# RMSNorm with swish on one core: load and store pieces regrouped at the start and the end

## Chip, cores and metric

One core of a Trainium2 chip. The metric is device microseconds of that core; most runs of a kernel lie within 0.3% of each other.

## The reference

```python
def reference(x, gamma, eps):            # x: [16, 1024, 512] float32, gamma: [512]
    rms = np.sqrt(np.mean(x ** 2, axis=-1, keepdims=True) + eps)
    x_norm = x / rms * gamma
    return (x_norm * (1.0 / (1.0 + np.exp(-x_norm)))).astype(np.float32)
```

16,384 rows of 512 floats (2 KB) go in and out: 33.55 MB each way. Spread over 128 partitions, that is 128 rows per partition; "a load of 16 rows" below means 16 rows in each partition, 4.19 MB in all.

## The kernel before

Data goes through a ring of 96 rows per partition. SyncE issues the loads, ScalarE the stores. Compute goes in chunks of 4 rows: ScalarE squares, VectorE (DVE) sums, GpSimd (POOL) makes the reciprocal root, VectorE normalises, ScalarE applies the swish in place, and the rows are stored from there. A load waits only for the stores of the rows whose place it takes.

```python
sizes = [4, 4, 8] + [16] * 6 + [8, 8]     # rows per partition of each tile: load = store
ring = 96
early = 2                                 # loads issued ahead of everything else
cn = 4                                    # rows per chunk
...
def dram(ap, t):                          # a tile is one contiguous block of HBM
    first, sz, _ = tiles[t]
    return ap[first : first + P * sz].rearrange("(p n) d -> p n d", n=sz)
...
def load(t):
    _, sz, at = tiles[t]
    ...                                   # waits: stores of tiles that held this place
    return nc.sync.dma_start(out=buf(t), in_=dram(xf, t)).then_inc(ld[t], 16)
...
def square(k):                            # ScalarE, chunk k
    t, at, first = chunks[k]
    if first:
        nc.scalar.wait_ge(ld[t], 16)      # the tile's load has landed
    ...
def store(t):
    need(
        nc.scalar.dma_start(out=dram(of, t), in_=buf(t)), s_swish, ends[t]
    ).then_inc(st[t], 16)
...
for k in range(K + 3):                    # ScalarE's program order
    if k < K:
        square(k)
    while stored < T and ends[stored] <= k - 2:
        store(stored)
        stored += 1
    if 2 <= k < K + 2:
        swish(k - 2)
```

Of the kernel before, what the change touches and what calls it, by code (L numbers as in the profile page):

```python
# [8 lines left out]
@with_exitstack  # L9
def kernel(  # L10
    ctx: ExitStack,
    tc: tile.TileContext,
    x: bass.AP,
    gamma: bass.AP,
    eps: bass.AP,
    out: bass.AP,
):
    nc = tc.nc
    P = nc.NUM_PARTITIONS
    AF = mybir.ActivationFunctionType  # L20
    ALU = mybir.AluOpType
    fp32 = mybir.dt.float32
    bf16 = mybir.dt.bfloat16

    xf = x.flatten_outer_dims()
    of = out.flatten_outer_dims()
    R, D = xf.shape


    sizes = [4, 4, 8] + [16] * 6 + [8, 8]  # L30
    ring = 96
    early = 2
    cn = 4
    n_sq = 3
    N = sum(sizes)
    assert N * P == R, (N, R)


    tiles = []
    done = 0  # L40
    for sz in sizes:
        assert done % ring + sz <= ring
        tiles.append((done * P, sz, done % ring))
        done += sz
    T = len(tiles)

    chunks = [
        (t, r, r == at)
        for t, (_, sz, at) in enumerate(tiles)
        for r in range(at, at + sz, cn)  # L50
    ]
    K = len(chunks)
    ends = []
    e = 0
    for sz in sizes:
        e += sz // cn
        ends.append(e)

    inv_d = 1.0 / float(D)
    eps_f = float(eps)  # L60



    tc.close()
    tc.compile()  # L65

    def sbuf(name, shape, dt=fp32):
        return nc.alloc_sbuf_tensor(name, shape, dt).ap()

    xb = sbuf("xb", [P, ring, D])  # L70
    gamma4 = sbuf("gamma4", [P, D])
    gamma_sb = sbuf("gamma_sb", [P, D])
    junk = [sbuf(f"junk{i}", [P, D], bf16) for i in range(2)]
    neg_half = sbuf("neg_half", [P, cn])
    ms = sbuf("ms", [P, K, cn])
    aeps = sbuf("aeps", [P, K, cn])
    rstd = sbuf("rstd", [P, K, cn])
    sq = [nc.alloc_psum_tensor(f"sq{i}", [P, 4, D], fp32).ap() for i in range(2)]

    ld = [nc.alloc_semaphore(f"ld{t}") for t in range(T)]  # L80
    st = [nc.alloc_semaphore(f"st{t}") for t in range(T)]
    scratch = nc.dram_tensor("scratch", [P, 16], fp32, kind="Internal").ap()
    blank = sbuf("blank", [P, 16])
    s_blank = nc.alloc_semaphore("s_blank")
    s_scratch = nc.alloc_semaphore("s_scratch")
    s_gld = nc.alloc_semaphore("s_gld")
    s_zero = nc.alloc_semaphore("s_zero")
    s_half = nc.alloc_semaphore("s_half")
    s_gamma = nc.alloc_semaphore("s_gamma")
    s_acc = nc.alloc_semaphore("s_acc")  # L90
    s_sq = nc.alloc_semaphore("s_sq")
    s_sum = nc.alloc_semaphore("s_sum")
    s_eps = nc.alloc_semaphore("s_eps")
    s_rstd = nc.alloc_semaphore("s_rstd")
    s_norm = nc.alloc_semaphore("s_norm")
    s_swish = nc.alloc_semaphore("s_swish")

    def need(ins, sem, value):
        return ins.wait_op(sem, value, "sem-ge")

    def dram(ap, t):
        first, sz, _ = tiles[t]
        return ap[first : first + P * sz].rearrange("(p n) d -> p n d", n=sz)

    def buf(t):
        _, sz, at = tiles[t]
        return xb[:, at : at + sz, :]


    stored_by_sync = set()  # L110

    def load(t):
        _, sz, at = tiles[t]
        waits = [
            u for u in range(t)
            if tiles[u][2] < at + sz and at < tiles[u][2] + tiles[u][1]
            and u not in stored_by_sync
        ]
        for u in waits:
            nc.sync.wait_ge(st[u], 16)  # L120
            stored_by_sync.add(u)
        return nc.sync.dma_start(out=buf(t), in_=dram(xf, t)).then_inc(ld[t], 16)

    entry = nc.main_func.blocks[0].instructions
    here = nc.cur_bb.bb.instructions
    for t in range(early):
        ins = load(t).ins
        assert here[-1] is ins or here[-1].name == ins.name
        here.pop()
        at = next(  # L130
            i for i, other in enumerate(entry)
            if other.engine == mybir.EngineType.SP
            and isinstance(other, mybir.InstDrain)
        )
        entry.insert(at, ins)
    for t in range(early, T):
        load(t)
    nc.sync.wait_ge(s_scratch, 16)


    nc.gpsimd.memset(blank, 0.0).then_inc(s_blank, 1)  # L141
    nc.gpsimd.memset(gamma4, 0.0).then_inc(s_zero, 1)  # L142
    nc.gpsimd.memset(neg_half, -0.5).then_inc(s_half, 1)  # L143
    nc.gpsimd.wait_ge(s_half, 1)
    for k in range(K):
        need(
            nc.gpsimd.tensor_scalar(  # L147
                out=aeps[:, k, :], in0=ms[:, k, :], scalar1=eps_f, scalar2=None,
                op0=ALU.add,
            ),  # L150
            s_sum, k + 1,
        ).then_inc(s_eps, 1)
        need(
            nc.gpsimd.tensor_tensor(  # L154
                out=rstd[:, k, :], in0=aeps[:, k, :], in1=neg_half, op=ALU.pow
            ),
            s_eps, k + 1,
        ).then_inc(s_rstd, 1)


    def square(k):
        t, at, first = chunks[k]
        if first:
            nc.scalar.wait_ge(ld[t], 16)
        acc = nc.scalar.activation(  # L165
            out=junk[k % 2], in_=xb[:, at + n_sq, :], func=AF.Square,
            scale=inv_d**0.5, accum_out=ms[:, k, n_sq : n_sq + 1],
        )
        if k >= 2:
            need(acc, s_acc, k - 1)  # L170
        acc.then_inc(s_acc, 1)
        square = nc.scalar.activation(  # L172
            out=sq[k % 2][:, 0:n_sq, :], in_=xb[:, at : at + n_sq, :],
            func=AF.Square, scale=inv_d**0.5,
        )
        if k >= 2:
            need(square, s_sum, k - 1)
        square.then_inc(s_sq, 1)

    def swish(k):  # L180
        _, at, _ = chunks[k]
        rows = xb[:, at : at + cn, :]
        need(
            nc.scalar.activation(out=rows, in_=rows, func=AF.Silu), s_norm, k + 1  # L184
        ).then_inc(s_swish, 1)

    def store(t):
        need(
            nc.scalar.dma_start(out=dram(of, t), in_=buf(t)), s_swish, ends[t]
        ).then_inc(st[t], 16)  # L190

    need(nc.scalar.dma_start(out=scratch, in_=blank), s_blank, 1).then_inc(
        s_scratch, 16
    )
    need(
        nc.scalar.dma_start(out=gamma4[0:P:32, :], in_=gamma.partition_broadcast(4)),
        s_zero, 1,
    ).then_inc(s_gld, 16)
    nc.scalar.preload_act_table_set("silu_and_others")  # L199
    stored = 0  # L200
    for k in range(K + 3):
        if k < K:
            square(k)
        while stored < T and ends[stored] <= k - 2:
            store(stored)
            stored += 1
        if 2 <= k < K + 2:
            swish(k - 2)


    def sums(k):
        need(
            nc.vector.tensor_reduce(  # L213
                out=ms[:, k, 0:n_sq], in_=sq[k % 2][:, 0:n_sq, :], op=ALU.add,
                axis=mybir.AxisListType.X,
            ),
            s_sq, k + 1,
        ).then_inc(s_sum, 1)

    def norm(k):  # L220
        _, at, _ = chunks[k]
        for j in range(cn):
            row = xb[:, at + j, :]
            ins = nc.vector.scalar_tensor_tensor(  # L224
                out=row, in0=row, scalar=rstd[:, k, j : j + 1], in1=gamma_sb,
                op0=ALU.mult, op1=ALU.mult,
            )
            if j == 0:
                need(ins, s_rstd, k + 1)
        ins.then_inc(s_norm, 1)  # L230

    for k in range(K + 1):
        if k < K:
            sums(k)
        if k == 0:
            need(
                nc.vector.stream_shuffle(gamma_sb, gamma4, [0] * 32), s_gld, 16  # L237
            ).then_inc(s_gamma, 1)
        if k == 1:
            nc.vector.wait_ge(s_gamma, 1)  # L240
        if k >= 1:
            norm(k - 1)


    for t in range(T):
        if t not in stored_by_sync:
            nc.sync.wait_ge(st[t], 16)

# [34 lines left out]
```

## Time and profile before

| | before |
|---|---|
| time | 160.27 us median of 3 (160.11 to 160.32) |
| span of the profiled run | 158.7 us |
| VectorE busy | 138.9 us, 87% |
| ScalarE busy | 125.3 us, 79% |
| moved | 67.15 MB, 423 GB/s over the span |
| loads / stores | 11 / 11 |
| last store | issued at 150.11, landed 8.6 us later |

Read the two limits together: VectorE runs without a gap from about 11 us on, but so do the DMA engines.

### The profile page before, as it was taken

The page shows a single profiled execution, that of the slowest core. Times are in us where ns is not written, and L with a number is a line of the kernel's source. Part 1 is how long each engine was busy: PE and PEld are TensorE (multiplying, and loading weights), DVE is VectorE, ACT ScalarE, POOL GpSimd, SP SyncE. Part 2 cuts the span into 40 slices and gives each one's busy share as a digit, 9 for nine tenths or more (in the row PEclk, how much of TensorE's full clock was granted, in tenths as well). Part 3 has the DMA queues.
Part 4 walks back from the last instruction along what each step waited for, and adds up shares of the span by engine and source line. Part 5 has one row for each costly group of instructions (what it writes and reads, how often), then busy time and mean ns, then how long its engine had stood idle before and what let it go on. Part 6 is the DMA issues. An engine that isn't in the chain of part 4 may idle for free.

```text
span 158.7 us, 439 instructions
## 1 busy us (share of the span) xinstructions
DVE 138.9 (87%) x162; ACT 125.3 (79%) x129; POOL 65.4 (41%) x71
## 2 busy tenths in 40 slices
DVE  0249999999999999999999999999999999999300
ACT  0935989888888889988888888888998888883600
POOL 2035444444455555544444445555544444445000
DMA  7999999999999999999999999999999999999997
GB/s 235 427 523 405 396 450 419 409 452 407 460 394 413 467 421 452 413 396 479 432 413 429 446 429 413 425 417 458 429 454 396 434 446 438 446 413 438 388 458 301
DMA packets 3324, 67.15 MB, mean 423 GB/s; under 512 B 501, under 2 KB 501, under 8 KB 505
## 3 DMA queue, kind: packets, MB, share of 16 engines
q1 hardware_dynamic: 1584, 33.56, 49.9%
q10 hardware_dynamic: 1736, 33.57, 49.3%
q14 instruction: 4, 0.02, 0.0%
HBM read 33.56 MB, written 33.56 MB: 423 GB/s over the span
## 4 chain that ended last, share of the span: by engine, by line
DVE 85%; DMA 5%; ACT 1%; issue 1%; POOL 0%; POOLq 0%
DVE xb L224 53%; DVE ms L213 32%; DMA gamma<-in_gamma_dram 5%; ACT xb L184 1%; DVE gamma_sb L237 0%; POOL gamma L142 0%; POOL blank L141 0%; POOLq L65 0%
## 5 line engine op out<-in xcount | busy, mean ns | idle before, releaser
L224 DVE SCALAR_TENSOR_TENSOR xb<-xb,rstd,gamma_sb 128x512 f32<-128x512 f32 x128 | 87.4, 748 | 0.0
L184 ACT ACTIVATE xb<-xb 128x2048 f32<-128x2048 f32 x32 | 61.1, 1909 | 17.8 <-DVE xb L224 17.8
L213 DVE TENSOR_REDUCE ms<-sq 128x3 f32<-128x1536 f32 x32 | 56.1, 1754 | 7.0 <-ACT sq L172 7.0
L147 POOL TENSOR_SCALAR aeps<-ms 128x4 f32<-128x4 f32 x32 | 20.6, 644 | 75.2 <-DVE ms L213 75.2
L172 ACT ACTIVATE sq<-xb 128x1536 f32<-128x1536 f32 x32 | 45.9, 1433 | 0.0
L154 POOL TENSOR_TENSOR rstd<-aeps,neg_half 128x4 f32<-128x4 f32 x32 | 44.0, 1376 | 2.7
L165 ACT ACTIVATE junk<-xb 128x512 bf16<-128x512 f32 x32 | 19.7, 615 | 3.4 <-DMA xb<-in_x_dram 3.3
L165 ACT ACTIVATION_READ_ACCUMULATOR junk<-xb 128x1 f32 x32 | 6.0, 186 | 0.0
L199 ACT ACT_TABLE_LOAD x1 | 1.3, 1283 | 3.6 <-issue 3.6
L237 DVE LOAD_MASK_SELECT gamma_sb<-gamma x1 | 0.0, 14 | 2.3 <-DMA gamma<-in_gamma_dram 2.3
L141 POOL MEMSET blank<- 128x16 f32 x1 | 0.1, 111 | 1.5 <-POOLq L65 1.5
L237 DVE STREAM_SHUFFLE gamma_sb<-gamma 128x512 f32<-128x512 f32 x1 | 0.7, 717 | 0.0
L142 POOL MEMSET gamma<- 128x512 f32 x1 | 0.5, 524 | 0.0
L264 POOL MEMSET const-float32-0.0<- 128x1 f32 x1 | 0.1, 98 | 0.2 <-issue 0.2
L264 POOL MEMSET const-bfloat16-1.0<- 128x1 bf16 x1 | 0.1, 102 | 0.0
L264 POOL MEMSET const-uint8-127<- 128x1 uint8 x1 | 0.1, 101 | 0.0
L143 POOL MEMSET neg_half<- 128x4 f32 x1 | 0.1, 101 | 0.0
L264 POOL MEMSET const-float32-1.0<- 128x1 f32 x1 | 0.1, 98 | 0.0
## 6 DMA issues: line engine op xcount, KB each, us to landing
xb<-in_x_dram SPq DMA_DIRECT2D x6, 4096.0 KB, 41.9
out_dram<-xb ACTq DMA_DIRECT2D x6, 4096.0 KB, 31.1
xb<-in_x_dram SPq DMA_DIRECT2D x3, 2048.0 KB, 35.0
out_dram<-xb ACTq DMA_DIRECT2D x3, 2048.0 KB, 10.7
xb<-in_x_dram SPq DMA_DIRECT2D x2, 1024.0 KB, 5.8
out_dram<-xb ACTq DMA_DIRECT2D x2, 1024.0 KB, 20.8
scratch<-blank ACTq DMA_DIRECT2D x1, 8.0 KB, 7.7
gamma<-in_gamma_dram ACTq DMA_DIRECT2D x1, 8.0 KB
```

What stands on the lines that cost most here:

```text
L141: nc.gpsimd.memset(blank, 0.0).then_inc(s_blank, 1)
L142: nc.gpsimd.memset(gamma4, 0.0).then_inc(s_zero, 1)
L147: nc.gpsimd.tensor_scalar(out=aeps[:, k, :], in0=ms[:, k, :], scalar1=eps_f, scalar2=None, op0=ALU.add,),
L154: nc.gpsimd.tensor_tensor(out=rstd[:, k, :], in0=aeps[:, k, :], in1=neg_half, op=ALU.pow),
L165: acc = nc.scalar.activation(out=junk[k % 2], in_=xb[:, at + n_sq, :], func=AF.Square, scale=inv_d**0.5, accum_out=ms[:, k, n_sq : n_sq + 1],)
L172: square = nc.scalar.activation(out=sq[k % 2][:, 0:n_sq, :], in_=xb[:, at : at + n_sq, :], func=AF.Square, scale=inv_d**0.5,)
L184: nc.scalar.activation(out=rows, in_=rows, func=AF.Silu), s_norm, k + 1
L199: nc.scalar.preload_act_table_set("silu_and_others")
L213: nc.vector.tensor_reduce(out=ms[:, k, 0:n_sq], in_=sq[k % 2][:, 0:n_sq, :], op=ALU.add, axis=mybir.AxisListType.X,),
L224: ins = nc.vector.scalar_tensor_tensor(out=row, in0=row, scalar=rstd[:, k, j : j + 1], in1=gamma_sb, op0=ALU.mult, op1=ALU.mult,)
L237: nc.vector.stream_shuffle(gamma_sb, gamma4, [0] * 32), s_gld, 16
L264: nc = _bacc.Bacc("TRN2", target_bir_lowering=False, num_devices=1)
```

## The change

The intent: fewer transfers. Rows are grouped as 8, 8 and seven times 16, and the pieces of loads and stores are listed apart from the groups. The first store moves 8 rows where it was two of 4; the last load moves 16 rows where it was two of 8. The first two loads (4 rows) and the last two stores (8 rows) keep their size, but are now pieces of a larger group, so in HBM each partition's piece lies at a pitch of 16 KB or 32 KB.

```diff
-    sizes = [4, 4, 8] + [16] * 6 + [8, 8]
+    groups = [8, 8] + [16] * 7
     ring = 96
+    loads = [(0, 0, 4), (0, 4, 4), (1, 0, 8)] + [(g, 0, 16) for g in range(2, G)]
+    stores = [(0, 0, 8), (1, 0, 8)] + [(g, 0, 16) for g in range(2, G - 1)]
+    stores += [(G - 1, 0, 8), (G - 1, 8, 8)]
     ...                                  # pieces are (group, first row, rows)
-    def dram(ap, t):
-        first, sz, _ = tiles[t]
-        return ap[first : first + P * sz].rearrange("(p n) d -> p n d", n=sz)
+    def dram(ap, piece):
+        g, r, n = piece
+        rows = ap[begin[g] * P : (begin[g] + groups[g]) * P]
+        return rows.rearrange("(p n) d -> p n d", n=groups[g])[:, r : r + n, :]
     ...
     def square(k):
-        t, at, first = chunks[k]
-        if first:
-            nc.scalar.wait_ge(ld[t], 16)
+        at, landing = chunks[k]          # the loads that this chunk is first to need
+        for i in landing:
+            nc.scalar.wait_ge(ld[i], 16)
```

The rest (cut) only carries the two lists through the ring waits, the semaphores and the final waits.

More of the change, by code (lines that the diff above doesn't have):

```diff
@@ L27 @@
     R, D = xf.shape
-    sizes = [4, 4, 8] + [16] * 6 + [8, 8]
+    groups = [8, 8] + [16] * 7
+    G = len(groups)
+    assert sum(groups) * P == R, R
+    begin = [sum(groups[:g]) for g in range(G)]
     ring = 96
+    loads = [(0, 0, 4), (0, 4, 4), (1, 0, 8)] + [(g, 0, 16) for g in range(2, G)]
+    stores = [(0, 0, 8), (1, 0, 8)] + [(g, 0, 16) for g in range(2, G - 1)]
+    stores += [(G - 1, 0, 8), (G - 1, 8, 8)]
     early = 2
@@ L34 @@
     n_sq = 3
-    N = sum(sizes)
-    assert N * P == R, (N, R)
-    tiles = []
-    done = 0
-    for sz in sizes:
-        assert done % ring + sz <= ring
-        tiles.append((done * P, sz, done % ring))
-        done += sz
-    T = len(tiles)
-    chunks = [
-        (t, r, r == at)
-        for t, (_, sz, at) in enumerate(tiles)
-        for r in range(at, at + sz, cn)
-    ]
-    K = len(chunks)
-    ends = []
-    e = 0
-    for sz in sizes:
-        e += sz // cn
-        ends.append(e)
+    chunks = []
+    new = list(range(len(loads)))
+    for g in range(G):
+        for c in range(0, groups[g], cn):
+            need_now = [
+                i for i in new if loads[i][0] == g and loads[i][1] < c + cn
+            ]
+            new = [i for i in new if i not in need_now]
+            chunks.append(((begin[g] + c) % ring, need_now))
+    assert not new
+    K = len(chunks)
+    ends = [-(-(begin[g] + r + n) // cn) for g, r, n in stores]
     inv_d = 1.0 / float(D)
@@ L78 @@
     sq = [nc.alloc_psum_tensor(f"sq{i}", [P, 4, D], fp32).ap() for i in range(2)]
-    ld = [nc.alloc_semaphore(f"ld{t}") for t in range(T)]
-    st = [nc.alloc_semaphore(f"st{t}") for t in range(T)]
+    ld = [nc.alloc_semaphore(f"ld{t}") for t in range(len(loads))]
+    st = [nc.alloc_semaphore(f"st{t}") for t in range(len(stores))]
     scratch = nc.dram_tensor("scratch", [P, 16], fp32, kind="Internal").ap()
@@ L99, in need, with buf, load @@
         return ins.wait_op(sem, value, "sem-ge")
-    def dram(ap, t):
-        first, sz, _ = tiles[t]
-        return ap[first : first + P * sz].rearrange("(p n) d -> p n d", n=sz)
-    def buf(t):
-        _, sz, at = tiles[t]
-        return xb[:, at : at + sz, :]
-    stored_by_sync = set()
-    def load(t):
-        _, sz, at = tiles[t]
-        waits = [
-            u for u in range(t)
-            if tiles[u][2] < at + sz and at < tiles[u][2] + tiles[u][1]
-            and u not in stored_by_sync
-        ]
-        for u in waits:
-            nc.sync.wait_ge(st[u], 16)
-            stored_by_sync.add(u)
-        return nc.sync.dma_start(out=buf(t), in_=dram(xf, t)).then_inc(ld[t], 16)
+    def dram(ap, piece):
+        g, r, n = piece
+        rows = ap[begin[g] * P : (begin[g] + groups[g]) * P]
+        return rows.rearrange("(p n) d -> p n d", n=groups[g])[:, r : r + n, :]
+    def buf(piece):
+        g, r, n = piece
+        at = (begin[g] + r) % ring
+        assert at + n <= ring
+        return xb[:, at : at + n, :]
+    stored_by_sync = set()
+    def load(i):
+        g, r, n = loads[i]
+        old = begin[g] + r - ring
+        for u, (h, q, m) in enumerate(stores):
+            if (
+                begin[h] + q < old + n and old < begin[h] + q + m
+                and u not in stored_by_sync
+            ):
+                nc.sync.wait_ge(st[u], 16)
+                stored_by_sync.add(u)
+        return nc.sync.dma_start(
+            out=buf(loads[i]), in_=dram(xf, loads[i])
+        ).then_inc(ld[i], 16)
     entry = nc.main_func.blocks[0].instructions
@@ L135 @@
         entry.insert(at, ins)
-    for t in range(early, T):
+    for t in range(early, len(loads)):
         load(t)
@@ L180, in swish @@
     def swish(k):
-        _, at, _ = chunks[k]
+        at, _ = chunks[k]
         rows = xb[:, at : at + cn, :]
@@ L188, in store @@
         need(
-            nc.scalar.dma_start(out=dram(of, t), in_=buf(t)), s_swish, ends[t]
+            nc.scalar.dma_start(out=dram(of, stores[t]), in_=buf(stores[t])),
+            s_swish, ends[t],
         ).then_inc(st[t], 16)
@@ L203 @@
             square(k)
-        while stored < T and ends[stored] <= k - 2:
+        while stored < len(stores) and ends[stored] <= k - 2:
             store(stored)
@@ L220, in norm @@
     def norm(k):
-        _, at, _ = chunks[k]
+        at, _ = chunks[k]
         for j in range(cn):
@@ L242 @@
             norm(k - 1)
-    for t in range(T):
+    for t in range(len(stores)):
         if t not in stored_by_sync:
```

## The prediction

> **What bounds the kernel now.** I read the page first for the busy shares, the memory rows and the chain that ended last. Then I asked for the landing of each transfer, and for the end of the timeline.
>
> The page of the kernel before:
>
> ```profile
> DVE  0249999999999999999999999999999999999300
> DMA  7999999999999999999999999999999999999997
> ...
> q1 hardware_dynamic: 1584, 33.56, 49.9%
> q10 hardware_dynamic: 1736, 33.57, 49.3%
> ...
> DVE 85%; DMA 5%; ACT 1%; issue 1%; POOL 0%; POOLq 0%
> ```
>
> The chain names VectorE (DVE, 85%), which runs without a gap from about 11 us to 148 us. But the DMA row is full in every slice, to the end. The two queues (q1 loads, q10 stores) fill 49.9 + 49.3 = 99.2% of 16 engines' 158.7 us. So two limits lie almost on one another, and the chain can name only one. Which one sets the end shows in the tail:
>
> ```profile
> 142.75 5.38 DVE L224 SCALAR_TENSOR_TENSOR xb<-xb,rstd,gamma_sb 128x512 f32<-128x512 f32 x8
> ...
> 148.17 1.91 ACT L184 ACTIVATE xb<-xb 128x2048 f32<-128x2048 f32 x1 [0.74 <-DVE xb L224]
> 150.11 0.34 ACTq L189 DMA_DIRECT2D out_dram<-xb  x1
> ```
> ```profile
> 144.00:148.00 4.00, 4.00 (x7) 1.91 (x1) 1.06 (x1) 1.00 0.96 414
> 148.00:152.00 4.00, 0.14 (x1) 1.91 (x1) 0.00 (x0) 1.00 0.95 406
> 152.00:156.00 4.00, 0.00 (x0) 0.00 (x0) 0.00 (x0) 1.00 1.06 455
> ```
>
> (The last columns of the second fence are the DMA share and GB/s.) The last store is issued at 150.11 and lands 8.6 us later, at 158.7. It carries 2.10 MB, which at 430 GB/s are 4.9 us. In the trace's packet records the store ahead of it is still moving until 153.4; only then does the last store get the engines, and its last packet ends at 158.3. A store into an empty queue would need some 1.5 to 2 us from issue to its first packet (the first load of all needs 1 us). So VectorE has a slack of about 3.3 - 1.8 = 1.5 us: **DMA throughput sets the end, VectorE is a close second.** 67.15 MB at the 430 GB/s of the middle of the run are 156 us, and the rest is start and receipt.
>
> **What the Trainium skill says.**
> - "DMA: Bandwidth & Descriptors", section "Where 436 GB/s comes from": the 16 ports together give 435 GB/s. The trace agrees: 421 to 441 GB/s in every stretch of 10 or 20 us between 30 and 140 us. So no cleverer order of transfers gains throughput.
> - Same page, "Queues, rings and completion order": each DMA engine goes round its queues packet by packet. Here a packet is one partition's row block: 1584 packets on q1 are 11 loads x (128 + 16 semaphore writes). So a queue with smaller packets gets a smaller share. Checked below against the landings, it agrees.
> - Same page, "Latency and other measured facts", HBM row pitch: pitches of 512 KiB and more, in powers of two, slow copies. The change makes the first two loads and the last two stores strided, with pitches of 16 and 32 KiB, far below that range; no run here shows yet what these cost.
>
> **The packet times, checked.** From the page, q10 moves 33.57 MB in 49.3% of 16 x 158.7 us, or 26.8 KB per us and engine: 0.31, 0.61 and 1.22 us for packets of 8, 16 and 32 KB (rows are 2 KB; 4, 8, 16 rows). An engine has 8 packets of each transfer. Alternating with 32 KB load packets a store of 4 rows takes 8 x (0.31 + 1.22) = 12.2 us, one of 8 rows 14.6, one of 16 rows 19.5. The first four stores, issued at 18.0, 22.5, 31.0 and 48.2:
>
> ```profile
> out_dram<-xb ACTq DMA_DIRECT2D x1, 1024.0 KB, 16.5
> out_dram<-xb ACTq DMA_DIRECT2D x1, 1024.0 KB, 25.0
> out_dram<-xb ACTq DMA_DIRECT2D x1, 2048.0 KB, 31.0
> out_dram<-xb ACTq DMA_DIRECT2D x1, 4096.0 KB, 33.1
> ```
>
> They land (last column, us after issue) at 34.5, 47.5, 62.0 and 81.3: spaced 13.0, 14.5, 19.3. The packet rule holds.
>
> **The change, part by part.**
>
> *Compute.* Nothing: 32 chunks of four rows, 128 normalising instructions of 748 ns, 32 sums of 1754 ns, the same waits between engines. No gain, no loss.
>
> *Start.* The same three first loads (4, 4, 8 rows), issued alike. Only the addresses of the first two are interleaved. VectorE's start hangs on gamma (landed at 11.0), which this does not touch. 0 us.
>
> *First store.* Two stores of 4 rows become one of 8, issued with the old second one at 22.5 instead of 18.0. Nothing idles meanwhile: the loads of the whole 96-row ring are queued by 4.9 us and the DMA row is full. But an 8-row packet gets a third of an engine where a 4-row one got a fifth. With the 4.3 us from issue to start that the first store showed, 22.5 + 4.3 + 14.6 = 41.4 us for the first landing, 56.0 for the second, against 62.0 for the same 16 rows before. The total rate is fixed, so the loads fall behind by what the stores gain: about 5.4 to 6 us of alternating.
>
> *Ring wait.* The load of rows 96 to 111 is issued when those stores land, so at 56 instead of 62. The load before it lands at about 82, so that wait was hidden, and stays hidden. 0 us.
>
> *Last load.* This is the part that could hurt. Before, the last three loads were
>
> ```profile
> xb<-in_x_dram SPq DMA_DIRECT2D x1, 4096.0 KB, 39.7
> ...
> xb<-in_x_dram SPq DMA_DIRECT2D x2, 2048.0 KB, 42.1
> ...
> xb<-in_x_dram SPq DMA_DIRECT2D x1, 2048.0 KB, 49.1
> ```
>
> (the middle line is the mean of the two small ones, 35.0 and 49.1). Issued at 62.1, 81.7 and 82.4, they land at 101.8, 116.7 and 131.5. The first 8 rows are wanted by ScalarE at 125.77 (its square of the 29th chunk), the other 8 at 134.4: slacks of 9 and 3 us. Now the 29th chunk waits for all 16 rows. The two small loads took 29.7 us, as 16 KB packets against 32 KB ones; one transfer of 32 KB packets takes 19.5, so it ends 10 us sooner, but the loads are 5.4 to 6 us late: 131.5 - 10.2 + 5.4 to 6 = **126.7 to 127.3**. My packet records give the same sum about 0.7 lower. ScalarE wants it at 125.77, and the VectorE sum behind it has another 0.33 us to spare (square ends 127.81, sum starts 128.14). So a stall of 0 to 1.2 us, most likely some 0.7 us.
>
> *End.* The last stores are of 16, 8 and 8 rows as before. A stall of 0.7 us moves the last issue from 150.1 to 150.8, inside the 1.5 us of slack. On the path: 0 us; if the load lands at 128.5 instead, some 2.4 - 1.5 = 0.9 us.
>
> *Packets.* One load and one store fewer: 2 x 144 = 288 packets of 3324, 18 per engine. In the packet records two 8 KB packets take 618 ns where one of 16 KB takes 611, two of 16 KB 1222 where one of 32 KB takes 1213, and a semaphore write 9. Saved per engine: 8 x 7 + 8 x 9 + 2 x 9 = 146 ns, on the path, as DMA sets the end: -0.15 us.
>
> Sum: 160.27 - 0.15 + a little for the chance of an unhidden stall (estimate 0.2) = 160.3 us.
>
> **The rivals.**
> 1. *The late last load becomes the bound.* For: the slack at its chunk falls from 9 us to about nothing. Against: the end has 1.5 us of slack, and its packets now take half of the engines, not a third. To cost 2% (3.2 us) it would have to land near 126.1 + 1.5 + 3.2 = 130.8, as late as all loads end now. Time then 161 to 163.
> 2. *Fewer, larger transfers gain.* For: DMA is the bound. Against: packets of 8 KB are already at full rate (0.309 us, 26.5 KB per us), and queues hide the fixed costs. At most 0.15 to 0.5 us: 159.8 to 160.1.
> 3. *The strided pieces or the later first store lose DMA time.* For: the first two loads meet an empty machine, and the last two stores are on the path. Against: packet lengths are unchanged, and the loads fill the gap. Ten per cent on the two last stores would be 1 us: 161.3.
>
> **Range and chances.** All that I can size lies between -0.5 and +1.2 us, and the three runs before lie within 0.2 us of each other. I take 159.7 to 161.4 as the range. Faster by 2% (157.1 us) would need over 435 GB/s on average: 1%. Slower by 2% (163.5) needs the worst case of rival 1 or something unseen: 2%. Within 2%: 97%.
>
> **What would show it.** DMA full in all slices again and about 430 GB/s in the middle; q1 with 1440 packets and q10 with 1592; first stores landing near 41 and 56; the last load landing near 127; a wait of ScalarE or VectorE of about a microsecond there, and VectorE ending near 149; the last store shorter from issue to landing by what VectorE lost (8.6 towards 7.9). It is wrong if the last load lands after 128.5, if the DMA row shows a hole near the end, or if the first or last slices move fewer GB/s than 235 and 301.

## The result

| | before | after |
|---|---|---|
| time, median | 160.27 us (160.11 to 160.32, 4 runs) | 160.34 us (160.24 to 160.80, 4 runs) |
| ratio | | 1.0011 (95%: 0.9991 to 1.0032) |
| span of the profiled run | 158.7 us | 158.9 us |

(Before has one more run here than in the table above.) A ratio is the mean time of one kernel's runs over that of the other's of the same rounds, so it isn't quite the ratio of the medians. The two kernels take the same time.

The page of the changed kernel: DMA busy tenths in 40 slices, the two queues (packets, MB, share of 16 engines), and the chain that ended last by engine.

```profile
DMA  7999999999999999999999999999999999999896
...
q1 hardware_dynamic: 1440, 33.56, 49.9%
q10 hardware_dynamic: 1592, 33.57, 49.1%
...
DMA 54%; DVE 34%; ACT 4%; issue 1%; POOL 0%; ACTq 0%; POOLq 0%
```

The DMA row is about as full as before, with the 288 packets fewer that were foretold. The chain now names DMA first, where it named VectorE with 85%. That looks like a new bottleneck and isn't: VectorE's busy time is 138.9 us in both. Near the end of the chain one chunk now waits for its load, so the walk back from the last instruction leaves VectorE there and follows the load and the stores behind it. A second trace of the same kernel (e11), with the same wait at the same chunk, names VectorE again:

```profile
DVE 83%; DMA 5%; ACT 4%; issue 1%; POOL 0%; another core or an unknown queue 0%; ACTq 0%; POOLq 0%
```

With two limits this close, the chain's shares tell which thread the walk picked up, not which limit holds.

That chunk in the timeline of the changed kernel (start, duration, engine, line, and in brackets the idle time before and what ended it), with the last store's issue:

```profile
126.33 0.63 ACT L169 ACTIVATE junk<-xb 128x512 bf16<-128x512 f32 x1 [0.33 <-DMA xb<-in_x_dram]
...
128.42 1.76 DVE L218 TENSOR_REDUCE ms<-sq 128x3 f32<-128x1536 f32 x1
...
150.40 0.34 ACTq L193 DMA_DIRECT2D out_dram<-xb  x1
```

ScalarE waits 0.33 us for the last load at the 29th chunk. VectorE's sum of that chunk starts at 128.42, where it was 128.14 before. But VectorE ran late before that: by 0.14 us at its first normalising (13.45, before 13.31) and by 0.08 us at the sum of the chunk ahead (123.91, before 123.83). So the late load costs it 0.2 us (0.21 in e11). The last store is issued 0.29 us later than before.

The first two stores and the last load of the changed kernel (KB, us from issue to landing):

```profile
out_dram<-xb ACTq DMA_DIRECT2D x1, 2048.0 KB, 19.4
...
out_dram<-xb ACTq DMA_DIRECT2D x1, 2048.0 KB, 26.2
...
xb<-in_x_dram SPq DMA_DIRECT2D x1, 4096.0 KB, 49.6
...
out_dram<-xb ACTq DMA_DIRECT2D x1, 2048.0 KB, 8.5
```

Issued at 22.47, 31.10 and 76.65, the first three land at 41.9, 57.3 and 126.2; foretold were 41.4, 56.0 and 126.7 to 127.3. The fourth line is the last store: 8.5 us, as against 8.6.

### The profile page after: what moved, and what is told of

It reads as the page before. It is cut to its first block, busy times and chain, and to the rows that moved or that the text cites. A ratio compares the mean times of both kernels' runs of the same rounds, so it can differ in the third digit from the quotient of the medians.

```text
span 158.9 us, 436 instructions
## 1 busy us (share of the span) xinstructions
DVE 138.9 (87%) x162; ACT 125.4 (79%) x129; POOL 90.1 (57%) x71
## 4 chain that ended last, share of the span: by engine, by line
DMA 54%; DVE 34%; ACT 4%; issue 1%; POOL 0%; ACTq 0%; POOLq 0%
DMA xb<-in_x_dram 31%; DVE xb L229 22%; DMA out_dram<-xb 18%; DVE ms L218 12%; DMA gamma<-in_gamma_dram 5%; ACT xb L188 2%; ACT sq L176 1%; ACT junk L169 0%; DVE gamma_sb L242 0%; POOL gamma L146 0%; POOL blank L145 0%; ACTq L168 0%; POOLq L64 0%
## 5 line engine op out<-in xcount | busy, mean ns | idle before, releaser
L151 POOL TENSOR_SCALAR aeps<-ms 128x4 f32<-128x4 f32 x32 | 50.5, 1577 | 50.9 <-DVE ms L218 50.9
L218 DVE TENSOR_REDUCE ms<-sq 128x3 f32<-128x1536 f32 x32 | 56.8, 1774 | 7.3 <-ACT sq L176 7.2
L158 POOL TENSOR_TENSOR rstd<-aeps,neg_half 128x4 f32<-128x4 f32 x32 | 38.8, 1212 | 2.7
```

The lines of the kernel that those rows point to most:

```text
L151: nc.gpsimd.tensor_scalar(out=aeps[:, k, :], in0=ms[:, k, :], scalar1=eps_f, scalar2=None, op0=ALU.add,),
L158: nc.gpsimd.tensor_tensor(out=rstd[:, k, :], in0=aeps[:, k, :], in1=neg_half, op=ALU.pow),
L218: nc.vector.tensor_reduce(out=ms[:, k, 0:n_sq], in_=sq[k % 2][:, 0:n_sq, :], op=ALU.add, axis=mybir.AxisListType.X,),
```

## The experiments

My theory: DMA throughput sets the end; the two queues share each DMA engine packet by packet, so packet sizes decide which queue runs ahead; and VectorE has a small slack at the end (time by which it may be late at no cost). Its rival: VectorE's chain sets the end, and a stall of it is paid in full. Landing times without a profile line below are those of the last semaphore write of a transfer in the trace's packet records, which are 0.4 to 1.1 us ahead of the landing in the profile.

### e1 to e4: the two parts apart, and the first store taken apart

e1 does the first part alone, e2 the second alone, e3 the second in the changed layout, e4 is e3 with both small stores held back:

```diff
 e1  groups = [8, 8] + [16] * 6 + [8, 8];  loads: (0,0,4), (0,4,4), then one per group;  stores: one per group
 e2  groups = [4, 4, 8] + [16] * 7;        loads: one per group;  stores: one per group, the last in two of 8
 e3  the changed kernel, with
-    stores = [(0, 0, 8), (1, 0, 8)] + ...
+    stores = [(0, 0, 4), (0, 4, 4), (1, 0, 8)] + ...
 e4  e3, and
+    ends[0] = ends[1]          # the first 4 rows wait for 8
```

> Only the first store is merged (8 rows at about 22.5 us); the last 16 rows are loaded as 8 and 8 again. My theory (queues share an engine packet by packet, DMA sets the end): the loads fall 5.1 us behind, as in the changed kernel (its last load ended at 125.8 in the packet records where 130.4 - 9.7 = 120.7 would be without it), so the very last load ends near 135.5 us instead of 130.4, ScalarE wants it at 134.4 and VectorE stalls about 1.3 us; the last store is issued near 151.4 instead of 150.1, which the drain of the store queue (it gets to the last store at 153.4) mostly hides: +0 to +0.3 us against before. Rival (VectorE's chain sets the end): the stall is on the path, +1.3 us or 0.8%.

> Only the last load is merged; stores of 4, 4, 8 rows at the start as before. My theory: the last load ends near 120.7 us in the packet records (130.4 - 9.7), some 5 us before ScalarE wants it, so no stall; VectorE ends at 148.2 as before; time within 0.2 us of before, about 0.1 us less for the fewer packets. Rival (a 16-row load in one transfer arrives later than two halves): a stall at the 29th chunk and a last issue after 150.1.

> The changed kernel with its first store split again into two of 4 rows (issued at 18.0 and 22.5), but with the changed layout: the first two loads and stores have 8 KB pieces at a pitch of 16 KB in HBM. Theory: a pitch costs nothing, so times and landings are those of e2 within 0.3 us (last load near 120.7). Rival (strided pieces cost DMA time): the first two loads land later than 4.5 and 6.9 us, or the whole is over 0.5 us slower than e2.

> As e3, but the first store of 4 rows waits for 8 rows, so both are issued at about 22.5. This parts the two halves of the first-store change: later, and in packets of 16 KB. Packet theory: the later start alone makes the stores 4 to 4.6 us later and the loads as much EARLIER, so the last load ends near 116.3 us, against 120.7 in e3 and 125.8 in the changed kernel. Rival (the later first store itself is what held the loads back): last load near or after 125.8. Time in both: within 0.3 us of before.

Measured, with 6 runs each and 11 of before on the same chip (median 160.36 us):

| | last load ends, expected | measured | time, median | ratio to before (95%) |
|---|---|---|---|---|
| e1 first store only | 135.5 | 135.9 | 160.86 | 1.0030 (0.9997 to 1.0062) |
| e2 last load only | 120.7 | 119.6 | 160.11 | 0.9982 (0.9954 to 1.0011) |
| e3 e2 in the changed layout | 120.7 | 121.1 | 160.44 | 1.0011 (0.9977 to 1.0046) |
| e4 e3, both stores late | 116.3 | 115.8 | 160.42 | 1.0003 (0.9970 to 1.0035) |
| before / changed kernel | | 130.4 / 125.8 | | |

Four landings, over a range of 20 us, come out within 1.1 us of what packet times, together with the landings of the two kernels, gave beforehand. e4 parts the first-store change in two: waiting longer brings the loads *forward* by 5.3 us (121.1 to 115.8); it's the 16 KB packets that push them back, by 10 us (115.8 to 125.8). The net of 4.7 us against e3 is what the prediction had as 5.4 to 6; e1 against before gives 5.5 for the same change.

Two expectations were missed in part. e3 was to match e2 within 0.3 us: its last load came 1.5 us later and its median is 0.33 us higher, and its first two loads ended at 4.80 and 7.31, past the 4.5 and 6.9 named for the rival (a cost of the pitch). The repeat of e2 (e12) ends its last load at 120.7, so a good part of the 1.5 us is scatter, and the intervals of e2 and e3 overlap: no cost of the pitch in time is shown, and one of a few tenths isn't excluded. In e2 VectorE ended at 148.91 and not at 148.2, because gamma landed late; its last store was issued at 150.88, 0.77 us later than before, and the span is still 158.8 us.

e1 is the stall test: the timeline of e1 at its 31st chunk, and its last issue.

```profile
136.30 0.63 ACT L168 ACTIVATE junk<-xb 128x512 bf16<-128x512 f32 x1 [1.54 <-DMA xb<-in_x_dram]
...
138.40 1.76 DVE L217 TENSOR_REDUCE ms<-sq 128x3 f32<-128x1536 f32 x1 [1.26 <-ACT sq L175]
...
151.74 0.34 ACTq L192 DMA_DIRECT2D out_dram<-xb  x1
```

VectorE stands still for 1.26 us (1.3 expected). The last store is issued at 151.74, yet lands 7.5 us after its issue instead of 8.6. In the packet records it follows the store ahead of it with no gap. The interval excludes the 0.8% of the rival, but e1's 0.3% can't be told from zero, nor from the 0.3 us that were allowed.

### e5: less VectorE work

```diff
-            row = xb[:, at + j, :]
+            row = xb[:, at + j, 0:384]
...
-                out=row, in0=row, scalar=rstd[:, k, j : j + 1], in1=gamma_sb,
+                out=row, in0=row, scalar=rstd[:, k, j : j + 1], in1=gamma_sb[:, 0:384],
```

> Wrong result on purpose: the changed kernel, but the normalising instructions work on 384 of 512 columns. VectorE loses some 0.17 us of each of 128 instructions, 20 us or more in all; ScalarE's work of about 3.9 us a chunk then paces the chunks at best. Theory (DMA throughput sets the end): same bytes, so the same time, between -0.7 and +1 us; the chunks now catch up with the loads and wait for them. Rival (VectorE's chain sets the end): 32 x 0.4 = 12 us or more faster.

Measured: 160.22 us against 160.13 of before, ratio 0.9986 (0.9935 to 1.0037). (The comparison with the reference let it pass: with this input gamma is 1 and the row factor near 1. It's still not the function wanted.) The page of e5, busy time and the rows of VectorE and DMA, then its 29th chunk from the timeline:

```profile
DVE 123.2 (78%) x162; ACT 124.5 (78%) x129; POOL 57.2 (36%) x71
...
DVE  0159978999999999999998499945999369997000
...
DMA  7999999999999999999999999999999999999896
```
```profile
126.25 0.63 ACT L169 ACTIVATE junk<-xb 128x512 bf16<-128x512 f32 x1 [3.64 <-DMA xb<-in_x_dram]
```

VectorE lost 15.7 us of work (138.9 to 123.2; I had expected 20 or more), and no gain in time shows (the interval reaches down to 1.0 us less). The work saved became holes in its row: ScalarE's squares waited 15.0 us for loads, in 7 places, against 3.9 us in the changed kernel. This is the clearest result: VectorE does not set the end. The rival wanted 12 us or more.

### e6: more bytes on the store queue

```diff
             store(stored)
+            if stored == 4:
+                nc.scalar.dma_start(out=extra,          # 1.05 MB, DRAM to DRAM
+                    in_=xf[0 : 4 * P].rearrange("(p n) d -> p (n d)", n=4),
+                ).then_inc(s_extra, 16)
```

> The changed kernel with 1.05 MB more on the store queue (a DRAM to DRAM copy of 8 KB per partition, issued behind the fourth store), on which nothing waits but the end. Theory (DMA has no idle time at all): 8 x 0.309 = +2.5 us. Rival (VectorE sets the end and DMA has room): below +1 us.

(In the kernel the copy stands behind the fifth store, not the fourth.) Measured: 163.10 us, ratio 1.0164 (1.0112 to 1.0216), that is +2.6 us (1.8 to 3.5), where 2.5 were expected. The first DMA engine to finish does so at 160.20 in the packet records, 157.63 in the changed kernel: +2.57. Within that interval, DMA time is paid one for one.

### e7 and e8: how much slack VectorE has

```diff
+        if k == K - 1:
+            for i in range(2):            # e8: range(6)
+                nc.vector.scalar_tensor_tensor(
+                    out=pad[:, i, :], in0=gamma_sb, scalar=rstd[:, 0, 0:1], in1=gamma_sb,
+                    op0=ALU.mult, op1=ALU.mult,
+                )
         for j in range(cn):
```

> The changed kernel with two more VectorE instructions of about 0.72 us ahead of the last four rows' normalising, which delays the last store's issue by 1.4 to 1.5 us, from 150.4 to 151.9. Theory: the store queue comes to the last store at 152.8 to 153.7 and a store needs 1.5 to 2 us from issue to first packet, so most of it is hidden: 0 to +0.6 us. Rival (the chain): +1.45 us, 0.9%.

> The same with six such instructions, 4.3 to 4.5 us: the last issue at about 154.8, well past the slack. Theory: +2.6 to +3.4 us, that is the delay less a slack of 1 to 1.8 us. Rival (the chain, no slack): +4.4 us.

Measured: e7 160.55 us, ratio 1.0013 (0.9965 to 1.0061); e8 162.15 us, ratio 1.0105 (1.0062 to 1.0147). e7 is hidden, as expected (the interval excludes the rival's 0.9%). e8 loses less than I expected: its span is 160.7 us, +1.8 on the changed kernel, not +2.6 to +3.4. The last store of e7, issued at 151.70, and that of e8, issued at 154.42:

```profile
out_dram<-xb ACTq DMA_DIRECT2D x1, 2048.0 KB, 7.3
```
```profile
out_dram<-xb ACTq DMA_DIRECT2D x1, 2048.0 KB, 6.3
```

Stretches of e8's tail (us, busy time of VectorE, ScalarE and GpSimd, then clock, DMA share and GB/s):

```profile
148.00:152.00 4.00, 4.00 (x7) 0.00 (x0) 0.00 (x0) 1.00 0.98 418
152.00:156.00 4.00, 0.45 (x1) 1.91 (x1) 0.00 (x0) 1.00 0.48 205
```

In e8 the queue has run empty (share 0.48), so 6.3 us is what this store takes when nothing stands before it. All above it is time spent in the queue, and so slack: 8.6 - 6.3 = 2.3 us before, 8.5 - 6.3 = 2.2 in the changed kernel, 1.2 left in e1, 1.0 in e7. e8's last issue is 4.02 us later than the changed kernel's, and 4.02 - 2.2 = 1.8 us is what it lost; that is the same two landings told once more, not a further check. A second way is: the store ahead ends at 153.43 (before) and 153.68 (changed kernel) in the packet records, and e8's last store needs 0.85 us from issue to first packet, so an issue up to 152.6 or 152.8 would have been in time. That is a slack of 2.4 to 2.5 us on the slowest engine.

### e9: the last load in four pieces, a miss

```diff
-    ... + [(g, 0, 16) for g in range(2, G)]
+    ... + [(g, 0, 16) for g in range(2, G - 1)]
+    loads += [(G - 1, r, 4) for r in (0, 4, 8, 12)]
```

> The opposite of the change's last load: the last 16 rows come in four loads of 4 rows (8 KB packets) in place of one of 16. Same bytes. Packet theory: against 32 KB store packets each of the four takes 8 x (0.31 + 1.22) = 12.2 us, so from 106.5 us they end near 118.7, 130.9, 143 and 151 (the last one sooner, as the stores run out of data), where ScalarE wants them at 126, 130.3, 134.7 and 139: VectorE stalls by some 12 us in all, the DMA row shows a hole near the end, and the time is 8 to 11 us longer. Rival (smaller pieces can be used sooner, the order of bytes is what counts): no stall, time within 0.5 us.

Measured: 161.08 us against 160.44 of before, ratio 1.0005 (0.995 to 1.0061); not 8 to 11 us longer. The pieces end at 119.4, 131.5, 137.8 and 140.2. The first two are where the packet rule has them (118.7 and 130.9); the last two come far sooner. The waits of ScalarE and the issue of a store between them, in the timeline of e9:

```profile
131.92 0.63 ACT L170 ACTIVATE junk<-xb 128x512 bf16<-128x512 f32 x1 [1.64 <-DMA xb<-in_x_dram]
...
138.18 0.63 ACT L170 ACTIVATE junk<-xb 128x512 bf16<-128x512 f32 x1 [2.37 <-DMA xb<-in_x_dram]
138.26 0.34 ACTq L194 DMA_DIRECT2D out_dram<-xb  x1
```

That store stands behind the square at 138.18 in ScalarE's program, so it's held by the very load that is late. In the packet records the store queue moves no data from 135.9 to 139.1, and the loads have the engines to themselves: they finish the third piece and take 2.45 us for the whole fourth (8 x 0.31), where alternating would have taken 12.2. My error was to let the store queue stay full: I counted stores as issued on time although ScalarE was waiting. A starved load heals itself here, because the queue that crowds it runs out of data. What is left is a VectorE stall of 1.37 + 1.85 us and, in the profiled run, a span of 160.0.

### e10 to e12: repeats

> The kernel before once more, for a second trace of its start and end. With pitch-free first loads the slowest of the 16 engines ended the first load at 4.45 us, 0.10 after the mean of the engines; in eight traces with the 16 KB pitch the slowest ended at 4.73 to 4.99, some 0.4 after the mean, with the same mean (4.32 to 4.40). If the pitch spreads the engines, this run shows 4.4 to 4.6 and a spread near 0.1 to 0.2; if it is chance, it can show 4.7 to 5.0.

> The changed kernel once more, timed with five rounds. Theory: ratio 0.998 to 1.003. Its first profile showed GpSimd's addition of eps at 1577 ns in the mean, where every other trace has some 644 ns; if that belongs to the kernel it comes again, if it was chance it is 644 again. The late last load (ScalarE waiting some 0.3 us at the 29th chunk) must come again in either case.

> The version with the last load merged and the first stores left as they were, timed on the same chip as the changed kernel. Theory: no stall at the 29th chunk, and a time within 0.3 us of the changed kernel, as both are bound by DMA throughput; 0.1 to 0.3 us less at best. Its first load has no pitch: as e10, the slowest engine ends it before 4.6 us if the pitch is what spreads the engines.

On one chip, with before at 160.12 us (11 runs): e11, the changed kernel, 160.42 us, ratio 1.0005 (0.9975 to 1.0034), its ScalarE waiting 0.41 us at the 29th chunk again; e12, the last load alone, 160.19, ratio 0.9986 (0.9952 to 1.0019), with no such wait. The end of the first load on the slowest engine: 4.44 in e10 and 4.46 in e12, both without the pitch; 4.67 in e11 with it. Over all traces it's 4.44 to 4.59 without the pitch (4 traces) and 4.67 to 4.99 with it (10 traces): no overlap. The mean over the engines is the same (4.14 to 4.35 and 4.32 to 4.40), so the slowest engine is later with the pitch, and the engines together aren't slower. That the pitch spreads them isn't shown: from their mean to the slowest it's 0.32 to 0.59 us with the pitch, 0.10 to 0.14 in three traces without it, but 0.45 in e2, which has none (my expectation for e10 left it out). Nothing waits on it for long: VectorE's start hangs on gamma, and the engines' mean end is 157.94 in both traces of before, and 157.92 and 157.96 in those of the changed kernel.

## Why the prediction was right

1. **The bound.** Right, and shown from both sides: e5 (15.7 us less VectorE work, no gain), e6 (1.05 MB more, +2.6 us).
2. **Compute and ring wait unchanged.** Right; VectorE is busy for 138.9 us in both, and the load that waits for the ring was issued at 57.4, long before the one ahead of it was done.
3. **The first store pushes the loads back.** Right, and in size about so: 4.7 us (e3 against the changed kernel) and 5.5 (before against e1), where I had 5.4 to 6. e4 shows why it happens: packet size, not the later issue.
4. **The last load arrives just about when it's wanted.** Right: 126.2 measured, 126.7 to 127.3 (or 0.7 less) foretold; the stall of VectorE is 0.2 us, inside the 0 to 1.2 given but under the 0.7 that I thought most likely. The two parts of the change pull against each other: together 125.8, alone 135.9 (e1) and 119.6 (e2).
5. **The stall is hidden.** Right, but the slack was mis-sized: I put the delay from issue to first packet at 1.5 to 2 us and got 1.5 us of slack. In e8's packet records that delay is 0.85 us (154.42 to 155.27), and the slack is 2.2 to 2.5 us. The same error made me expect too much of e8. It did no harm here, as the stall was far below either figure.
6. **0.15 us for fewer packets.** Not seen in the time, and too small for these runs to see. In the first traces the packets' durations add up to 0.11 us less per engine (157.29 against 157.40 us), but the repeats turn it round (157.40 in e11, 157.17 in e10). The last semaphore write of the run stands at 158.55 against 158.30, because the slowest engine ended 0.6 us after the mean and not 0.4; the repeats ended at 158.47 (before) and 158.74 (after). The pitch of the last stores doesn't decide that: e4, with it, ended at 158.36, and e1, without it at the end, at 158.91.
7. **A sign of being wrong that showed.** I had called the prediction wrong if the last slice moved less than 301 GB/s. The changed kernel moved 280 there, in both traces. That would fit rival 3 (strided pieces lose DMA time), but doesn't speak for it: the repeat of before moved 297, e1, whose last stores have no pitch, 263, and e2, which has it, 314. The sign was too tight for the scatter of one slice.
8. **The number.** 160.3 us against 160.34 is closer than runs of one kernel agree (160.24 to 160.80), so that closeness is luck; what the runs bear out is that the two kernels take the same time.

The version with the last load alone had a ratio below 1 both times (0.9982 in e2, 0.9986 in e12), but both intervals contain 1. No version was shown to beat both kernels. With the DMA engines nine tenths busy or more in nearly every slice, there was little for a rearrangement to gain.

## What to carry to other kernels

Where nearly every slice of the DMA row was full, regrouping transfers moved waits about but not the end. So first size the slack, as the last store's time from issue to landing less the same store's time into an empty queue. Where a load queue and a store queue were both full, the smaller packet lost (e4, e9); enlarging a piece on one queue delayed the other, so look for the chunk that waits for it. In e9 the loss stopped when the favoured queue ran out of data.

## What the Trainium skill lacked or had wrong

- "DMA: Bandwidth & Descriptors", "Queues, rings and completion order", has the round robin by packet, but not its consequence: with two full queues the shares go as the packet sizes, and what the profile counts as a packet was a whole partition's row block. Here such packets were 8, 16 and 32 KB (309, 611 and 1213 ns). Against 32 KB packets a load of 4 rows took 12.1 us (e9, 119.4 to 131.5) and alone 2.45 us.
- Same page, "Latency and other measured facts", gives some 600 ns to the first byte for the path that ScalarE's stores take, and speaks of a fixed cost of some 2 us, but of none for this path alone. For a 2.10 MB store into an empty queue e8 shows 0.85 us from the start of the issuing instruction (itself 0.34 us) to the first packet, and 6.3 us in all, of which 8 x 0.611 = 4.9 us are packets: 1.4 us fixed. On small HBM pitches the section says nothing. Here a pitch of 16 KB left the mean end of the first load's engines alone (4.32 to 4.40 us against 4.14 to 4.35), while the slowest ended at 4.67 to 4.99 against 4.44 to 4.59.
- No page says how far apart the 16 engines of one transfer end. In the last store the first and the last engine were 0.75 and 1.1 us (before, e10), 0.9 and 1.1 us (after, e11) and 2.3 us (e3) apart; e3's profiled run took 161.57 us, where its median is 160.44.
- "SBUF — State Buffer", "Who interferes with whom", says that a VectorE instruction with two SBUF inputs contends with a GpSimd instruction that reads SBUF. The changed kernel's first trace fits that in part: beside four such VectorE instructions without a gap a GpSimd addition, else of 0.66 us, took 2.65 us and ended just after the fourth. In that trace it came with every chunk from 65 us to the wait at the 29th, twice in e11, and cost VectorE no wait. But it's 17 of the 434 times that the addition started beside four such instructions in all traces; the other 417, in which VectorE had started first too, took 0.52 to 0.67 us, and these runs don't say what decides.

```profile
65.20 2.76 DVE L229 SCALAR_TENSOR_TENSOR xb<-xb,rstd,gamma_sb 128x512 f32<-128x512 f32 x4
65.40 2.65 POOL L151 TENSOR_SCALAR aeps<-ms 128x4 f32<-128x4 f32 x1 [2.19 <-DVE ms L218]
```
